# A fused two-layer decoder trunk: small loads wait for the input stream, filler matmuls follow the first real ones, token combinations go behind the first weights

## The chip, the cores and the metric

The kernel runs on one core of a Trainium2 chip. Its engines are TensorE (PE in the tables: matrix products), VectorE (DVE), ScalarE (ACT), GpSimd (POOL) and SyncE (SP, which here only issues transfers). Sixteen DMA engines move data between memory (HBM) and the on-chip buffers. The metric is the device time of one execution in microseconds (us), as the median of several runs; lower is better.

## What is computed

The reference is a trunk of two layers over 512 tokens with 1024 features, in float32. Each layer adds three parts to x; a last normalisation follows.

```python
D_MODEL = 1024; SEQ = 512; D_FF = 2816
# even layer: x += 0.5*SwiGLU(rms(x)); x += Wout[A(.) || B(.)](rms(x)); x += 0.5*SwiGLU(rms(x))
#    A = dilated sliding-window attention, B = sparse attention over indexed keys
# odd layer:  x += 0.5*SwiGLU(rms(x)); x += Wout C(rms(x)); x += 0.5*SwiGLU(rms(x))
#    C = sliding-window (128) grouped-query attention with sinks
# final RMSNorm; one relative-position bias table is added to the logits of A, B and C
```

SwiGLU(h) is (silu(h w1) * (h w3)) w2, with 2816 hidden features. So the trunk is four feed-forwards, two attentions between them and a normalisation.

## The kernel before

All of x stays on chip, as eight chunks of 128 features by 512 tokens (`self.x`). A float32 operand is split into a high and a low part (the high one is a cast by ScalarE, L336, the low one a subtraction by VectorE, L315), and a product is three matmuls: L366 to L368 in the plain form, L581 to L583 in the form with seven products.

**A feed-forward** (`ffn`) takes the 22 blocks of 128 hidden features in parts of 8, 8 and 6 (`PARTS`). The first four blocks (`PLAIN`) of the first part are computed by `gate` with plain matmuls: for each block a bank of results for w1 and one for w3, eight chunks of x by three matmuls, 24 in a bank. So there are eight plain banks. They work on x before its normalisation factor is known; `rms` finds that factor meanwhile (`newton` is its chain of small steps on VectorE), and each bank is multiplied by it afterwards (L450, L452, product L453). The other blocks come in pairs through `gates`, which forms two-by-two blocks of tokens and weights and saves one product in eight. It needs combinations of the normalised tokens (`normed`: L471 normalises a chunk, L493 adds or subtracts halves of chunks on VectorE or GpSimd, and each result is split) and of the weights (`sevens`: L533 adds halves, again on either engine). L594 copies the results out on ScalarE and L597 adds on VectorE. At the end of a part w2 is multiplied on.

**The attentions** read bias rows from a table in memory. `tables` makes it in the first feed-forward: GpSimd's queue loads its inputs, stores the rows (`rv`), and copies them shifted to `tab0` and `tab1` (the issues `tab<-rv`). A head's rows are then loaded by `toeplitz` (L661) into a buffer of kind `toep`, on SP's queue.

**The order** is a list that `Plan.emit` writes. Each operation has a due value v, the costs that the plan holds for it, and the engines that may run it; the plan repeatedly takes the engine that can start earliest and, on it, the ready operation with the least v. `CAPACITY`, `LIMIT` and `RESERVE` bound how many buffers of a kind are held. What this list fixes is the order on each engine; on the chip each engine runs its own list in order and waits by semaphores. So a transfer that can't be issued holds up all those behind it on SP's queue. `setup` issues the eight chunks of x and the first constants (ident, the identity matrix; cqg and gcol, scale vectors), and begins with a warm-up block: `WARM` = 12 matmuls on a buffer of zeros (L1045).

Of the kernel before, what the change touches and what calls it, by code (L numbers as in the profile page):

```python
# [36 lines left out]
LIMIT = {'mm': 4, 'sc': 2, 'sci': 4, 'pt': 2, 'ptv': 1, 'o': 6, 'tmp': 6, 'relu': 2, 'score': 3, 'qx': 6, 'toep': 5, 'prob': 6, 'turn': 3, 'sq': 2, 'q': 4, 'k': 4, 'vf': 3, 'of': 4, 'gt': 16, 'wraw': 6, 'cq2': 2, 'xn': 10, 'sa': 2, 'sb': 2, 'sk': 2}  # L37
RESERVE = {'q': 8, 'vf': 4, 'whl': 3, 'wraw': 5}


# [75 lines left out]
class Plan:  # L116
# [55 lines left out]
    def emit(self, make):  # L172
# [11 lines left out]
        free = {t: [0.0] * n for t, n in CAPACITY.items()}  # L184
        held, turn = {}, {}

        def offer(o):
# [4 lines left out]
        def slot_time(o):  # L192
            t, need = 0.0, {}
            for b in o.alloc:
                if held.get(b.kind, 0) + need.get(b.kind, 0) >= LIMIT.get(b.kind, 1 << 30):
                    return None
                if b.rank != turn.get(b.kind, 0) + need.get(b.kind, 0):
                    return None
                need[b.kind] = need.get(b.kind, 0) + 1
                n = need[b.tag, 0] = need.get((b.tag, 0), 0) + 1  # L200
                f = free[b.tag]
                if len(f) < n + RESERVE.get(b.kind, 0):
                    return None
                t = max(t, f[n - 1])
            return t
# [5 lines left out]
        while count < total:  # L211
# [30 lines left out]
            for b in o.alloc:  # L242
# [5 lines left out]
                b.t = make(b)  # L248
            fn()
            now[e] = st + ns  # L250
            o.fin, o.eng, o.done = st + ns + o.lat, e, True
# [16 lines left out]
class Trunk:  # L268
# [87 lines left out]
    def matmuls(self, ps, hl, rhs, m=128, c0=0, step=None):  # L356

        nc = self.nc
        n = len(rhs)
        for i, (xh, xl) in enumerate(rhs):  # L360
            c = c0 + i * (step or m)

            def f(i=i, c=c, xh=xh, xl=xl):
                o = ps.t[:m]
                wh, wl = hl.at(0, slice(c, c + m)), hl.at(1, slice(c, c + m))
                nc.tensor.matmul(o, wl, xh.t, start=i == 0, stop=False)  # L366
                nc.tensor.matmul(o, wh, xl.t, start=False, stop=False)  # L367
                nc.tensor.matmul(o, wh, xh.t, start=False, stop=i == n - 1)  # L368
            self.pe(3 * pe_ns(S), f, self.parts(hl, i, n) + [xh, xl], [ps])

    def hi(self, out, src, rows=slice(None), key=None, sb=True, n=S):
# [44 lines left out]
    def rms(self, n):  # L416
# [11 lines left out]
        def f3():  # L428
            for tb in range(4):
                nc.tensor.transpose(p2.t[:, tb * 128:(tb + 1) * 128], y.t[:, tb:tb + 1].to_broadcast([128, 128]),  # L430
                                    self.ident)
        self.pe(1000, f1, [acc, "ident"], [p1], v0)
        self.dve(2300, lambda: list(self.newton(p1.t[:, :4], y.t, n)), [p1], [y], v0)
        self.pe(450, f3, [y], [p2], v0)
        self.act(act_ns(S, False), lambda: nc.scalar.copy(r.t, p2.t), [p2], [r], v0)
# [22 lines left out]
    def normed(self, R, ncol):  # L458
# [29 lines left out]
        def comb(o, i, a, j, b, k, add=False):  # L488
# [6 lines left out]
            self.p.op([("dve", vec_ns(256), f(nc.vector)), ("pool", 750.0, f(nc.gpsimd))], keys, [(o, i)], v)  # L495
        top, low, ts = [], [], []
        for k in range(4):
# [4 lines left out]
        for k in range(4):  # L502
            low.append(norm(k + 4))
            both(["b21", "b22"], slot(), low[k], slice(0, 512), slice(0, 512), (), [low[k]])
        for k in range(4):
            a, x0, x1 = self.s2("xn"), top[k], low[k]
            ts.append(a)
            comb(a, 0, x0, 0, x0, 1)
# [338 lines left out]
    def hybrid(self, nxt):  # L847
# [13 lines left out]
        for m in range(2):  # L861
# [4 lines left out]
            self.act(act_ns(S, True, 1), lambda f=f, ch=ch, g=g: nc.scalar.activation(  # L866
                ch.t, f.t, AF.Copy, scale=g), [f, "g"], [ch])
            self.dve(dve_ns(S), lambda f=f, ch=ch, cl=cl, g=g: nc.vector.scalar_tensor_tensor(
# [160 lines left out]
    def setup(self):  # L1029
# [13 lines left out]
        ps = self.bank("ptv")  # L1043
        for _ in range(WARM):
            self.pe(427, lambda: nc.tensor.matmul(ps.t, idle[:, :128], idle, start=True, stop=True), ["idle"], [ps], v)  # L1045
        self.act(1500, lambda: nc.scalar.activation(idle2, idle[:, :1], AF.Square), ["idle"], ["idle2"], v)
        self.dma(lambda: nc.scalar.dma_start(self.gcol, t["gcol"]), (), ["g0"], 28672, v, "act")
        self.dma(lambda: nc.scalar.dma_start(self.cqg, t["cqg"]), ["g0"], ["g"], 1024, v, "act")
        self.dma(lambda: nc.scalar.dma_start(self.ident, t["ident"]), (), ["ident0"], 65536, v, "act")
        self.dve(50, lambda: nc.vector.memset(self.ones, 1.0), ["ident0"], ["ident"], v)  # L1050
        self.x = [self.s2("x") for _ in range(KD)]
        for k, x in enumerate(self.x):
            self.dma(lambda k=k, x=x: nc.sync.dma_start(x.t, t["x"][k]), (), [x], 262144, START_X[k])

    def tables(self):
# [6 lines left out]
        v = LATE  # L1062
        self.dma(lambda: pool.dma_start(self.tri, t["tri"]), (), ["tri"], 65536, v, "pool")
        self.act(250, lambda: nc.scalar.copy(self.identb, self.ident), ["ident"], ["identb"], v)
        self.dma(lambda: pool.dma_start(self.sinkp, bass.AP(
            tensor=t["sinks"].tensor, offset=t["sinks"].offset, ap=[[0, 128], [1, 16]])), (), ["sink0"], 8192, v, "pool")
        self.dve(80, lambda: nc.vector.tensor_scalar(self.sinkn, self.sinkp, -1.0, 0.0, op0=OP.mult, op1=OP.add),
                 ["sink0"], ["sink"], v)
        self.dma(lambda: pool.dma_start(tab.t, t["table"]), (), [tab], 2048, v, "pool")
        for c0, (a, n) in enumerate(((0, 512), (512, TOEP - 512))):  # L1070
            self.dma(lambda c0=c0, a=a, n=n: pool.dma_start(hot[c0].t[:, :n], t["onehot"][:, a:a + n]), (), [hot[c0]],
                     65536, v, "pool")
# [3 lines left out]
            for i in range(2):  # L1076
                ad, rs = add[2 * c0 + i], res[2 * c0 + i]
                self.dma(lambda i=i, a=a, n=n, ad=ad: pool.dma_start(ad.t[:, :n], t["addc"][:, i, a:a + n]), (), [ad],
                         32768, v, "pool")
# [69 lines left out]
    def norm_half(self, part, acc, sq):  # L1149
# [7 lines left out]
        def f1():  # L1157
            for i in range(2):
                tb = slice((2 * part + i) * 128, (2 * part + i) * 128 + 128)
                nc.tensor.matmul(p1.t[:, i:i + 1], acc.t[:, tb], self.ones, start=True, stop=False)  # L1160
                nc.tensor.matmul(p1.t[:, i:i + 1], sq.t[:, tb], self.ones, start=False, stop=True)
        self.pe(700, f1, [acc, (sq, part), "ident"], [p1], v0)
        steps = []
# [76 lines left out]
LATE = 20000.0  # L1240
WARM = 12
START_X = (-20000.0, -16900.0, -11000.0, -10900.0, -9000.0, -8900.0, -6000.0, -5900.0)

# [78 lines left out]
```

## Time and profile before

| | us |
|---|---|
| median of 3 runs | 1855.19 (1854.97 to 1855.77) |
| the profiled execution | 1856.36 |
| its span in the trace | 1854.6 |

The profiled execution is 1.76 us longer than its span, and 1.17 us above the median. Times in the trace count from the start of the span. The granted clock is given as a share: 1.00 is 2.4 GHz for TensorE and 0.50 is 1.2 GHz. A row of a timeline gives the start, the duration, engine, source line and operation, and in brackets the idle time before it with what ended it. In the trace's names `d` is a buffer of 128 x 1024, `s` one of 128 x 512, `ps` a bank of results.

### The profile page before, as it was taken

How to read it: one execution, taken by the hardware profiler on the slowest of the kernel's cores; microseconds unless marked ns; L12 is line 12 of the kernel's file. 1: busy time of each engine (PE TensorE's matmuls, PEld its weight loads, DVE VectorE, ACT ScalarE, POOL GpSimd, SP SyncE). 2: the span in 40 equal slices, each digit the busy share in tenths (PEclk: the TensorE clock that was granted, in tenths of full speed). 3: DMA queues.
4: the chain of work that ended last, by engine and by line, in shares of the span. 5: the costliest groups of instructions: out<-in, count | busy, mean ns of one | idle time of the engine just before them, and what ended most of it. 6: DMA issues, size and time to landing. Idle time of an engine off the chain costs nothing.

```text
span 1854.6 us, 28373 instructions
## 1 busy us (share of the span) xinstructions
PE 1811.5 (98%) x11174; PEld 1619.7 (87%) x11178; DVE 1398.2 (75%) x2222; ACT 936.2 (50%) x1558; POOL 245.1 (13%) x240
## 2 busy tenths in 40 slices
PE   8899999989999999999999999999999999999997
PEld 6789989867877789899998989989888889899896
DVE  7965866759998898487588965857789898567483
ACT  6443533636757746254264543525569655345153
POOL 1500001024622120010001000001023120010010
PEclk9899999999999999999999999999999999999999
DMA  6463233432222323234334223323412223243131
GB/s 210 121 207 101 84 101 106 126 103 77 87 59 78 93 71 121 62 108 132 91 103 125 69 91 103 125 70 103 137 60 69 86 80 95 78 124 126 60 112 46
DMA packets 65431, 185.45 MB, mean 100 GB/s; under 512 B 11985, under 2 KB 14769, under 8 KB 65297
## 3 DMA queue, kind: packets, MB, share of 16 engines
q1 hardware_dynamic: 58176, 176.88, 30.9%
q0 software_dynamic: 6688, 6.66, 1.3%
q8 instruction: 87, 1.43, 0.3%
q14 instruction: 48, 0.39, 0.1%
q10 hardware_dynamic: 432, 0.10, 0.0%
HBM read 179.81 MB, written 8.47 MB: 102 GB/s over the span
## 4 chain that ended last, share of the span: by engine, by line
PE 81%; DVE 12%; issue 2%; ACT 2%; DMA 2%; POOL 1%; SPq 1%; DVEq 0%; POOLq 0%; ACTq 0%
PE ps L581 12%; PE ps L582 12%; PE ps L583 12%; PE ps L366 11%; PE ps L367 11%; PE ps L368 11%; DVE d L315 3%; DVE s L315 2%; PE ps L837 1%; DMA d<-in_w 1%; PE ps L839 1%; PE ps L838 1%; PE ps L797 1%; DVE s L755 1%; DVE s L471 1%
## 5 line engine op out<-in xcount | busy, mean ns | idle before, releaser
L336 ACT CAST d<-d 128x1024 fp32r<-128x1024 f32 (+4 forms) x492 | 448.6, 927 | 405.0 <-DMA d<-in_w 223.3
L315 DVE TENSOR_TENSOR d<-d,d 128x1024 fp32r<-128x1024 f32 (+3 forms) x475 | 507.1, 1084 | 176.1 <-ACT d L336 155.0
L581 PE MATMUL ps<-s,d 128*128 128x256 f32 x2016 | 572.2, 284 | 10.9 <-DVE d L315 7.9
L582 PE MATMUL ps<-s,d 128*128 128x256 f32 x2016 | 571.5, 283 | 0.0
L583 PE MATMUL ps<-s,d 128*128 128x256 f32 x2016 | 571.4, 283 | 0.0
L366 PE MATMUL ps<-s,d 128*128 128x512 f32 x1188 | 471.8, 397 | 3.6 <-DVE d L315 3.6
L367 PE MATMUL ps<-s,d 128*128 128x512 f32 x1188 | 465.1, 392 | 0.2
L368 PE MATMUL ps<-s,d 128*128 128x512 f32 x1188 | 464.7, 391 | 0.0
L581 PEld LDWEIGHTS ps<-s,d 128*128 128x128 f32 x2016 | 388.0, 192 | 12.5 <-DVE d L315 8.2
L582 PEld LDWEIGHTS ps<-s,d 128*128 128x128 f32 x2016 | 388.0, 192 | 0.5
L583 PEld LDWEIGHTS ps<-s,d 128*128 128x128 f32 x2016 | 387.9, 192 | 0.0
L366 PEld LDWEIGHTS ps<-s,d 128*128 128x128 f32 x1188 | 224.4, 189 | 47.9 <-DVE d L315 3.8
L368 PEld LDWEIGHTS ps<-s,d 128*128 128x128 f32 x1188 | 224.0, 189 | 47.8
L367 PEld LDWEIGHTS ps<-s,d 128*128 128x128 f32 x1188 | 224.5, 189 | 42.9 <-DVE s L315 0.5
L594 ACT COPY d<-ps 128x512 f32<-128x512 f32 x144 | 84.4, 586 | 217.6 <-PE ps L583 217.5
L653 DVE SCALAR_TENSOR_TENSOR s<-ps,s 128x512 f32<-128x512 f32 x88 | 60.7, 690 | 137.0 <-PE ps L368 136.8
L315 DVE TENSOR_TENSOR s<-s,s 128x512 fp32r<-128x512 f32 (+2 forms) x188 | 148.7, 803 | 7.3 <-ACT s L372 2.1
L533 POOL TENSOR_TENSOR d<-d 128x512 f32<-128x512 f32 x18 | 23.6, 1313 | 937.1 <-DVE d L533 807.1
L597 DVE TENSOR_TENSOR d<-ps,d 128x512 f32<-128x512 f32 x108 | 73.5, 686 | 32.7 <-PE ps L583 32.1
L533 DVE TENSOR_TENSOR d<-d,d 128x512 f32<-128x512 f32 x133 | 87.5, 686 | 1.7
L533 DVE TENSOR_TENSOR d<-d 128x512 f32<-128x512 f32 x126 | 85.6, 695 | 2.2
L764 ACT ACTIVATE s<-s,stat 128x256 f32<-128x256 f32 (+3 forms) x128 | 65.9, 516 | 24.6 <-DVE stat L755 23.9
(147 smaller groups left out, 1872.0 us busy)
## 6 DMA issues: line engine op xcount, KB each, us to landing
d<-in_w SPq DMA_DIRECT2D x234, 512.0 KB, 3.7
d<-in_w SPq DMA_DIRECT2D x32, 384.0 KB, 3.2
d<-in_hyb_in SPq DMA_DIRECT2D x22, 512.0 KB, 3.9
d<-in_swa_in SPq DMA_DIRECT2D x10, 512.0 KB, 3.6
tab<-rv POOLq DMA_DIRECT2D x4, 1024.0 KB, 16.7
s<-tab SPq DMA_DIRECT2D x16, 256.0 KB, 4.0
d<-in_hyb_out SPq DMA_DIRECT2D x16, 256.0 KB, 2.9
d<-in_swa_out SPq DMA_DIRECT2D x16, 256.0 KB, 2.7
```

The lines of the kernel that those rows point to most:

```text
L315: return lambda: eng.tensor_sub(out(), a(), b().bitcast(F32))
L336: alts = [("act", ns[0](n), lambda: nc.scalar.copy(hl.at(0, o), raw.t[:, c]))]
L366: nc.tensor.matmul(o, wl, xh.t, start=i == 0, stop=False)
L367: nc.tensor.matmul(o, wh, xl.t, start=False, stop=False)
L368: nc.tensor.matmul(o, wh, xh.t, start=False, stop=i == n - 1)
L533: return lambda: eng.tensor_add(o.t[:, oc], a.t[:, ac], o.t[:, oc])
L581: nc.tensor.matmul(o, wl, xh, start=start and m == 0 and k == 0, stop=False, skip_group_check=True)
L582: nc.tensor.matmul(o, wh, xl, start=False, stop=False, skip_group_check=True)
L583: nc.tensor.matmul(o, wh, xh, start=False, stop=k == 3, skip_group_check=True)
L594: self.act(sca_ns(S) - 40, lambda: nc.scalar.copy(view(q, c), bank(ps)), [ps], [(q, key)])
L597: self.dve(vec_ns(S), lambda: nc.vector.tensor_add(view(q, c), bank(ps), view(q, c)), [ps, (q, key)], [(q, key)])
L764: nc.scalar.activation(x, x, AF.Exp, bias=st.t[:, qb:qb + 1], scale=-1.0, accum_out=st.t[:, 4 + qb:5 + qb])
```

## The change

There are five edits. A `toep` buffer is handed out only if its load is due at most 30 us (30000 in the plan's units) after the latest matmul that was put on the list (`AHEAD`, `front`). Six more matmuls on zeros (`FILL`) follow the first three real ones, in the bank of the warm-up block. The token combinations in `normed` get a due value 22 us later, in all four feed-forwards. The loads of ident and cqg move from ScalarE's queue to GpSimd's, and with those of tri, sinks, table, onehot and addc wait until the sixth chunk of x has landed. The memset of the ones no longer waits for ident.

```diff
+AHEAD = {'toep': 30000.0}
...
+                if b.kind in AHEAD and o.v > front + AHEAD[b.kind]:
+                    return None
...
             fn()
+            if e == "pe":
+                front = max(front, o.v)
...
             self.pe(3 * pe_ns(S), f, self.parts(hl, i, n) + [xh, xl], [ps])
+            if self.warm and i == 0:
+
+                self.warm(FILL, self.parts(hl, i, n) + [xh, xl], self.vt)
+                self.warm = None
...
+
+        v += 22000.0
         for k in range(4):
             a, x0, x1 = self.s2("xn"), top[k], low[k]
-            ts.append(a)
             comb(a, 0, x0, 0, x0, 1)
...
-        self.dma(lambda: nc.scalar.dma_start(self.cqg, t["cqg"]), ["g0"], ["g"], 1024, v, "act")
-        self.dma(lambda: nc.scalar.dma_start(self.ident, t["ident"]), (), ["ident0"], 65536, v, "act")
-        self.dve(50, lambda: nc.vector.memset(self.ones, 1.0), ["ident0"], ["ident"], v)
+        self.dve(50, lambda: nc.vector.memset(self.ones, 1.0), (), ["ones"], v)
...
-            self.dma(lambda k=k, x=x: nc.sync.dma_start(x.t, t["x"][k]), (), [x], 262144, START_X[k])
+            self.dma(lambda k=k, x=x: nc.sync.dma_start(x.t, t["x"][k]), (), [x, ("landed", k)], 262144, START_X[k])
+
+        self.dma(lambda: nc.gpsimd.dma_start(self.ident, t["ident"]), [("landed", 5)], ["ident"], 65536, 0.0, "pool")
...
-        self.dma(lambda: pool.dma_start(self.tri, t["tri"]), (), ["tri"], 65536, v, "pool")
+        after = [("landed", 5)]
+        self.dma(lambda: pool.dma_start(self.cqg, t["cqg"]), after, ["cqg"], 1024, v, "pool")
+        self.dma(lambda: pool.dma_start(self.tri, t["tri"]), after, ["tri"], 65536, v, "pool")
...
+FILL = 6
```

The plan decides the rest, so the order on the engines is shown at three places. Numbers in the names tell buffers apart and differ between the two kernels; line numbers of the changed kernel are higher by 7 to 17.

On TensorE, at the end of the warm-up block, three real matmuls followed one another before, on one bank:

```order
L1045 MATMUL ps<-idle 128x512
L366 MATMUL ps<-s_125,d_122 128x512
L367 MATMUL ps<-s_131,d_114 128x512
L368 MATMUL ps<-s_125,d_114 128x512
L366 MATMUL ps<-s_125,d_137 128x512
L367 MATMUL ps<-s_131,d_129 128x512
L368 MATMUL ps<-s_125,d_129 128x512
```

Now the first three (L373 to L375) are followed by six on zeros (two are shown, each with its weight load):

```order
L1058 MATMUL ps<-idle 128x512
L373 MATMUL ps<-s_102,d_117 128x512
L374 MATMUL ps<-s_110,d_107 128x512
L375 MATMUL ps<-s_102,d_107 128x512
L1058 LDWEIGHTS idle
L1058 MATMUL ps<-idle 128x512
L1058 LDWEIGHTS idle
L1058 MATMUL ps<-idle 128x512
```

The fills stand between the first chunk of x and the next matmul; before, that next matmul worked on the w3 weight with the same chunk.

On VectorE, ahead of the first products of `gates`, the split of the second weight (w3, a row of L315 with 128x1024) stood at place 77, after token combinations (L493) and their splits:

```order
L493 TENSOR_TENSOR s_535<-s_501,s_460 128x256
L315 TENSOR_TENSOR s_538<-s_486,s_519 128x512
L315 TENSOR_TENSOR s_543<-s_489,s_540 128x512
L493 TENSOR_TENSOR s_535<-s_535,s_460 128x256
L315 TENSOR_TENSOR s_563<-s_491,s_558 128x512
L315 TENSOR_TENSOR s_568<-s_499,s_565 128x512
L315 TENSOR_TENSOR s_574<-s_501,s_570 128x512
L1080 TENSOR_TENSOR s_579<-s_510,ps 16x512
L315 TENSOR_TENSOR d_583<-d_297,d_398 128x1024
```

Now it stands at place 70, after the rescaling of one more plain bank pair (L461 to L464, before L450 to L453):

```order
L482 SCALAR_TENSOR_TENSOR s_484<-s_160,gcol,s_376 128x512
L1097 TENSOR_TENSOR s_499<-s_255,ps 16x512
L461 TENSOR_TENSOR s_508<-ps,s_376 128x512
L463 TENSOR_TENSOR s_514<-ps,s_376 128x512
L322 TENSOR_TENSOR s_520<-s_484,s_506 128x512
L464 TENSOR_TENSOR s_514<-s_508,s_514 128x512
L322 TENSOR_TENSOR d_537<-d_295,d_413 128x1024
L322 TENSOR_TENSOR s_547<-s_514,s_539 128x512
```

On TensorE all eight plain banks now stand ahead of the first product (L593); before, 48 products stood between the sixth and the seventh. The w1 split of the second group of `gates` is VectorE's 93rd row before and its 99th now.

On SP's queue, in the first feed-forward, loads of bias rows (L661) stood between the weights (L328):

```order
L328 DMA d_692<-in_w 128x1024
L661 DMA s_858<-tab_69 128x512
L328 DMA d_875<-in_w 128x1024
L661 DMA s_893<-tab_69 128x512
L661 DMA s_908<-tab_69 128x512
L661 DMA s_911<-tab_69 128x512
L328 DMA d_927<-in_w 128x1024
```

Now only weights (L335) stand there:

```order
L335 DMA d_755<-in_w 128x1024
L335 DMA d_764<-in_w 128x1024
L335 DMA d_895<-in_w 128x1024
L335 DMA d_961<-in_w 128x1024
L335 DMA d_981<-in_w 128x1024
```

The first loads of bias rows moved to just before the first attention uses them, and those of the other table to the second attention's input projections.

## Rows read from the trace of the kernel before

**Rows 1.** The page: TensorE's busy time, its share of the span, instructions.

```profile
PE 1811.5 (98%) x11174; PEld 1619.7 (87%) x11178; DVE 1398.2 (75%) x2222; ACT 936.2 (50%) x1558; POOL 245.1 (13%) x240
```

**Rows 2.** TensorE's waits over the span: total us, times, longest.

```profile
PE ps L581 <- DVE d L315: 7.9, 1, 7.9
```

**Rows 3.** Timeline of TensorE, 0 to 17 us: start, duration.

```profile
1.20 5.07 PE L1045 MATMUL ps<-idle 128*128 128x512 bf16 x12 [1.20 <-DVE ones L1050]
...
7.43 0.39 PE L368 MATMUL ps<-s,d 128*128 128x512 f32 x1
11.15 0.80 PE L366 MATMUL ps<-s,d 128*128 128x512 f32 x1 [3.32 <-DVE d L315]
...
16.30 0.40 PE L366 MATMUL ps<-s,d 128*128 128x512 f32 x1
16.54 0.39 PE L367 MATMUL ps<-s,d 128*128 128x512 f32 x1
```

**Rows 4.** Timeline of ScalarE, 0 to 16 us.

```profile
9.75 0.62 ACT L336 CAST d<-d 128x512 fp32r<-128x512 f32 x1 [3.50 <-DMA d<-in_w]
```

**Rows 5.** DMA, 0 to 16 us: GB/s by 0.4 us; an issue, us to landing.

```profile
GB/s 0 0 0 0 41 134 364 362 300 379 254 217 141 89 105 85 171 264 222 247 247 323 391 410 394 307 302 384 353 405 410 394 405 384 384 384 389 379 384 364
...
tri<-in_tri POOLq DMA_DIRECT2D x1, 64.0 KB, 5.2
```

**Rows 6.** Windows: length; busy us of PE, PEld, DVE, ACT, POOL; clock; DMA share; GB/s.

```profile
4.00:7.20 3.20, 2.85 (x8) 0.90 (x7) 1.38 (x2) 1.44 (x3) 0.11 (x1) 1.00 0.92 166
...
10.00:16.00 6.00, 4.85 (x11) 3.81 (x12) 5.04 (x9) 5.31 (x10) 0.00 (x0) 0.50 1.05 375
...
31.80:72.85 41.05, 33.17 (x158) 27.47 (x157) 39.15 (x53) 20.00 (x33) 26.43 (x23) 0.88 0.10 30
...
450.00:550.00 100.00, 96.66 (x488) 79.77 (x488) 99.12 (x254) 58.68 (x130) 52.13 (x47) 1.00 0.25 76
```

**Rows 7.** Timeline of TensorE, 59 to 76 us.

```profile
59.13 0.58 PE L581 MATMUL ps<-s,d 128*128 128x256 f32 x1 [7.88 <-DVE d L315]
59.51 0.41 PE L582 MATMUL ps<-s,d 128*128 128x256 f32 x1
...
63.77 0.35 PE L581 MATMUL ps<-s,d 128*128 128x256 f32 x1
...
75.63 0.28 PE L581 MATMUL ps<-s,d 128*128 128x256 f32 x1
75.74 0.28 PE L582 MATMUL ps<-s,d 128*128 128x256 f32 x1
```

**Rows 8.** Timeline of VectorE, 28 to 78 us.

```profile
31.80 2.36 DVE L315 TENSOR_TENSOR d<-d,d 128x1024 fp32r<-128x1024 f32 x2
...
34.78 0.68 DVE L452 TENSOR_TENSOR s<-ps,s 128x512 f32<-128x512 f32 x1
35.38 0.74 DVE L471 SCALAR_TENSOR_TENSOR s<-s,gcol,s 128x512 f32<-128x512 f32 x1
...
42.48 1.22 DVE L471 SCALAR_TENSOR_TENSOR s<-s,gcol,s 128x512 f32<-128x512 f32 x1
...
70.58 2.34 DVE L315 TENSOR_TENSOR d<-d,d 128x1024 fp32r<-128x1024 f32 x2
```

**Rows 9.** Timeline of SP's queue, 0 to 100 us.

```profile
11.68 52.84 SPq L328 DMA_DIRECT2D d<-in_w  x17
88.70 0.33 SPq L661 DMA_DIRECT2D s<-tab  x1
```

**Rows 10.** Timeline of ScalarE, 95 to 104 us.

```profile
101.77 1.05 ACT L336 CAST d<-d 128x1024 fp32r<-128x1024 f32 x1 [1.57 <-DMA d<-in_w]
```

**Rows 11.** TensorE's waits, 0 to 110 us: total, times, longest.

```profile
PE ps L581 <- ACT d L594: 1.7, 2, 1.0
```

**Rows 12.** Timeline of TensorE at 1543 us.

```profile
1543.39 0.39 PE L581 MATMUL ps<-s,d 128*128 128x256 f32 x1 [1.30 <-ACT d L594]
```

**Rows 13.** Waits of SP's queue over the span: total, times, longest.

```profile
SPq L328 <- DVE d L315: 541.7, 99, 18.3
```

More of the change, by code (lines that the diff above doesn't have):

```diff
@@ L185, in emit @@
         held, turn = {}, {}
+        front = -1.0e9
         def offer(o):
@@ L431, in f3 @@
                                     self.ident)
-        self.pe(1000, f1, [acc, "ident"], [p1], v0)
+        self.pe(1000, f1, [acc, "ones"], [p1], v0)
         self.dve(2300, lambda: list(self.newton(p1.t[:, :4], y.t, n)), [p1], [y], v0)
-        self.pe(450, f3, [y], [p2], v0)
+        self.pe(450, f3, [y, "ident"], [p2], v0)
         self.act(act_ns(S, False), lambda: nc.scalar.copy(r.t, p2.t), [p2], [r], v0)
@@ L495, in comb @@
             self.p.op([("dve", vec_ns(256), f(nc.vector)), ("pool", 750.0, f(nc.gpsimd))], keys, [(o, i)], v)
-        top, low, ts = [], [], []
+        top, low = [], []
         for k in range(4):
@@ L866, in hybrid @@
             self.act(act_ns(S, True, 1), lambda f=f, ch=ch, g=g: nc.scalar.activation(
-                ch.t, f.t, AF.Copy, scale=g), [f, "g"], [ch])
+                ch.t, f.t, AF.Copy, scale=g), [f, "cqg"], [ch])
             self.dve(dve_ns(S), lambda f=f, ch=ch, cl=cl, g=g: nc.vector.scalar_tensor_tensor(
@@ L1043, in setup, with warm @@
         ps = self.bank("ptv")
-        for _ in range(WARM):
-            self.pe(427, lambda: nc.tensor.matmul(ps.t, idle[:, :128], idle, start=True, stop=True), ["idle"], [ps], v)
+        def warm(n, r, v):
+            for _ in range(n):
+                self.pe(427, lambda: nc.tensor.matmul(ps.t, idle[:, :128], idle, start=True, stop=True), ["idle", *r], [ps], v)
+        self.warm = warm
+        warm(WARM, (), v)
         self.act(1500, lambda: nc.scalar.activation(idle2, idle[:, :1], AF.Square), ["idle"], ["idle2"], v)
-        self.dma(lambda: nc.scalar.dma_start(self.gcol, t["gcol"]), (), ["g0"], 28672, v, "act")
-        self.dma(lambda: nc.scalar.dma_start(self.cqg, t["cqg"]), ["g0"], ["g"], 1024, v, "act")
-        self.dma(lambda: nc.scalar.dma_start(self.ident, t["ident"]), (), ["ident0"], 65536, v, "act")
-        self.dve(50, lambda: nc.vector.memset(self.ones, 1.0), ["ident0"], ["ident"], v)
+        self.dma(lambda: nc.scalar.dma_start(self.gcol, t["gcol"]), (), ["g"], 28672, v, "act")
+        self.dve(50, lambda: nc.vector.memset(self.ones, 1.0), (), ["ones"], v)
         self.x = [self.s2("x") for _ in range(KD)]
         for k, x in enumerate(self.x):
-            self.dma(lambda k=k, x=x: nc.sync.dma_start(x.t, t["x"][k]), (), [x], 262144, START_X[k])
+            self.dma(lambda k=k, x=x: nc.sync.dma_start(x.t, t["x"][k]), (), [x, ("landed", k)], 262144, START_X[k])
+        self.dma(lambda: nc.gpsimd.dma_start(self.ident, t["ident"]), [("landed", 5)], ["ident"], 65536, 0.0, "pool")
     def tables(self):
@@ L1062, in tables @@
         v = LATE
-        self.dma(lambda: pool.dma_start(self.tri, t["tri"]), (), ["tri"], 65536, v, "pool")
+        after = [("landed", 5)]
+        self.dma(lambda: pool.dma_start(self.cqg, t["cqg"]), after, ["cqg"], 1024, v, "pool")
+        self.dma(lambda: pool.dma_start(self.tri, t["tri"]), after, ["tri"], 65536, v, "pool")
         self.act(250, lambda: nc.scalar.copy(self.identb, self.ident), ["ident"], ["identb"], v)
         self.dma(lambda: pool.dma_start(self.sinkp, bass.AP(
-            tensor=t["sinks"].tensor, offset=t["sinks"].offset, ap=[[0, 128], [1, 16]])), (), ["sink0"], 8192, v, "pool")
+            tensor=t["sinks"].tensor, offset=t["sinks"].offset, ap=[[0, 128], [1, 16]])), after, ["sink0"], 8192, v, "pool")
         self.dve(80, lambda: nc.vector.tensor_scalar(self.sinkn, self.sinkp, -1.0, 0.0, op0=OP.mult, op1=OP.add),
                  ["sink0"], ["sink"], v)
-        self.dma(lambda: pool.dma_start(tab.t, t["table"]), (), [tab], 2048, v, "pool")
+        self.dma(lambda: pool.dma_start(tab.t, t["table"]), after, [tab], 2048, v, "pool")
         for c0, (a, n) in enumerate(((0, 512), (512, TOEP - 512))):
-            self.dma(lambda c0=c0, a=a, n=n: pool.dma_start(hot[c0].t[:, :n], t["onehot"][:, a:a + n]), (), [hot[c0]],
+            self.dma(lambda c0=c0, a=a, n=n: pool.dma_start(hot[c0].t[:, :n], t["onehot"][:, a:a + n]), after, [hot[c0]],
                      65536, v, "pool")
@@ L1077, in tables @@
                 ad, rs = add[2 * c0 + i], res[2 * c0 + i]
-                self.dma(lambda i=i, a=a, n=n, ad=ad: pool.dma_start(ad.t[:, :n], t["addc"][:, i, a:a + n]), (), [ad],
+                self.dma(lambda i=i, a=a, n=n, ad=ad: pool.dma_start(ad.t[:, :n], t["addc"][:, i, a:a + n]), after, [ad],
                          32768, v, "pool")
@@ L1161, in f1 @@
                 nc.tensor.matmul(p1.t[:, i:i + 1], sq.t[:, tb], self.ones, start=False, stop=True)
-        self.pe(700, f1, [acc, (sq, part), "ident"], [p1], v0)
+        self.pe(700, f1, [acc, (sq, part), "ones"], [p1], v0)
         steps = []
```

## The prediction

> **What bounds the kernel now.** I read the page first: TensorE (PE) is busy for 98% of the span [rows 1]. So a change can win only where PE waits or runs at the lower of its two clocks, and I went to PE's waits next: the list by line, for the span, comes to some 30 us, and one wait makes 7.9 of them [rows 2]. Then I followed each wait that the edits touch back to what is late. The reader is to see three places.
>
> The start: PE's first three real matmuls end at 7.83, and the next starts at 11.15 [rows 3]. ScalarE sat 3.50 us waiting for a weight, till 9.75 [rows 4]. The DMA engines were busy all that time, but the rate sank to 85 to 141 GB/s in four slices of 0.4 us, where it is near 390 later [rows 5]. The small loads are in flight there: 64 KB of tri took 5.2 us. From 10 to 16 us the granted clock is 0.50 [rows 6], that is 1.2 GHz, after the 3.32 us gap; the twelve matmuls from 11.15 to 16.30 stand 0.43 apart, then 0.23 [rows 3].
>
> The first feed-forward: PE stops at 51.25 for 7.88 us and comes back at half clock, 0.213 us a product for 21 products, against 0.12 later [rows 7]. What it waited for is the w3 split that VectorE (DVE) did just ahead of 59.13; the order shows it behind token combinations.
>
> The second half of that stage: SP issues nothing from 64.5 to 88.70, where a toep load waits for its table [rows 9]; three w2 weights are issued behind it. ScalarE then waits for w2, once 1.57 us [rows 10]; a copy (L594) stands behind those casts, and two waits of PE on that copy make 1.7 us of the first 110 [rows 11].
>
> **The change part by part.** *Start.* The small loads leave the first 5 us; they start when the sixth chunk of x is there. With no slump a 256 KB piece should land every 0.65 us (390 GB/s [rows 5]), so the weight needed at 9.73 comes near 5.5. PE's first real matmul hangs on the warm-up block, which ends at 6.27 [rows 3], and hardly moves. Six fills follow: at 0.213 (half of the 0.42 that the twelve at 1.2 GHz took, 5.07/12 [rows 3]) 1.3 us, at 0.42 2.5 us. The matmul that began at 16.30 is the 16th; 7.83 + 1.3 + 12 x 0.23 = 11.9. So the start gains 4.4, and with the first matmul 0.2 earlier 4.6. Bounds: 1.0, if the fills don't hold the clock (twelve matmuls at 0.43 and fills at 0.42 give back 3.6), and 5.0.
>
> *Token combinations behind the first weights.* In the new order the w3 split stands at DVE's 70th place and not at its 77th, so the 7.88 us wait goes. But all eight plain banks (192 matmuls) now stand ahead of the first product, before it were six, and DVE evacuates two more banks early. What is late next is the second weight group: its w1 split was DVE's 93rd row and is its 99th. Before, from the end of the newton steps at 31.80 to the end of that split at 71.72, which is the first of the two from 70.58 [rows 8], DVE took 39.9 us; in this stretch it was nearly always busy (39.15 of 41.05 us [rows 6]). The new list has four more rescalings of a bank (L450, L452) and one more multiplication (L453), two more splits of 512, one more small subtraction, one weight sum of two halves more and two in-place ones less, no L597: at 0.6 from start to start [rows 8] that is 4 x 0.6 + 0.6 + 2 x 0.6 + 0.2 - 0.6 - 0.6 = 3.2. So the split ends 43.1 us after newton, which ends at 31.80 - 4.6 = 27.2: 70.3. PE could be there at 75.63 - 4.6 - 7.9 - 2.0 = 61.1 (2.0: the 21 slow products at 0.093 more each). So there is a new wait, of some 9 us, in place of the old one, and the clock falls again. The products of the second group start at 70.3 and not at 75.63 [rows 7], 5.3 earlier; the half-clock stretch, which was over by 75.63, is now still to come: less 2.0, a gain of **3.3**.
>
> The unknown in this is how much GpSimd (POOL) slows DVE. With POOL idle an L471 took 0.74 us, with POOL at its combinations 1.22 [rows 8], and POOL was busy 26.43 of the 41.05 us [rows 6]. Instruction by instruction, against those of the same kind with POOL idle, I count some 7.7 us of such excess in the old stretch. Its combinations are the same twelve, so I leave it as it is. Bounds: an excess of 2 us gives 5.7 more, one of 13 takes 5.3 off. The Trainium skill's page "SBUF — State Buffer", section "SBUF: two separate sides", states that a DVE instruction with two SBUF inputs and a GpSimd one share a port pair that one holds for its whole instruction while the other is blocked. By that rule moving the combinations can't remove the excess, only put it elsewhere; the rows agree as far as they go, and a sum by the rule, with each of twelve combinations holding DVE for its own 1.2 us, would put the split at about 77, no gain.
>
> The other three feed-forwards get the same offset. In the one at 1500 a copy stands behind two casts and PE waits 1.30 [rows 12]; the copy moves ahead of them: **1.3**, bounds 0 and 1.3.
>
> *Toep buffers near the front.* SP's block of 24 us goes, since no toep load is left in the first feed-forward; what hid behind it, the w2 weights, come early, and the two waits on the copy go [rows 11]: **1.7**, bounds 0 and 1.7. The loads go to 360 to 380 us and, for the other table, to the second attention. There SP's queue is in order, and a weight ahead of a toep load waits for its buffer, up to 18.3 us [rows 13]. I cost it at nothing: what covers it is the 30 us by which they are let in ahead of PE. Small swaps in the first attention (450 to 550, DVE busy 99.12 of 100 us [rows 6]) have no cover there: between -3 and +3, taken at 0.
>
> Sum: 3.3 + 1.3 + 1.7 = 6.3 us. The profiled execution took 1856.36 with a span of 1854.6; that is 1.17 above the median of the runs, so I take the sum off the median: 1855.19 - 6.3 = **1848.9**.
>
> **Rivals.**
> (1) *The start gains and DVE eats it.* The second group's split comes at 73.6 or later (73.6 + 2.0 = 75.63): the excess would have to be 11 us. For it: POOL has an add more in this stage, and DVE rows 82 to 99, about 10 us, wait for banks of the last plain part. Against it: POOL's combinations are as many as before. Then only 1.3 + 1.7 remain: 1852.2, and with one of these missing no difference.
> (2) *The slump moves and does not go.* The Trainium skill's page "DMA: Bandwidth & Descriptors", section "Issuing engines are not separate DMA queues", states that transfers of all engines run on the same 16 DMA engines and interleave, so that a queue change alone frees nothing. As a mechanism of this kernel: the slump cost (375 - 166) GB/s x 3.2 us [rows 6], 0.67 MB or 1.8 us of stream, and after the sixth chunk it falls on the weights of the second plain bank, needed at 18 to 24 us. Against it: SP fetches those weights well ahead of need once nothing holds it. If so, the start gains 2.8, the sum is 4.5, the time 1850.7.
> (3) *Slower: one toep load is stuck.* In the second attention a toep load issued behind a weight that waits for its buffer comes too late. SP's longest such wait is 18.3 us [rows 13]; if PE meets all of it: 18.3 - 6.3 = 12.0, 1867. It decides from 10 us of lateness on. For it: before, those loads were done hundreds of us ahead. Against it: 30 us ahead of PE is more than 18.3, and PE has other work there.
> (4) *Better.* The excess on DVE is small since its w3 split and evacuations run while POOL still waits: split at 64 to 66, the wait at the second group 3 to 5 us, the clock mostly kept: 5 more, 1844.
>
> **How the numbers follow.** A difference under 0.2%, 3.7 us, is about what a measurement of this kernel can't tell from none: the edges are 1851.5 and 1858.9. Chances: my forecast 0.42 and (2) 0.11, nearly all of it faster; (4) 0.14, faster; (1) 0.18, nearly all within 0.2%; (3), with all other ways of losing (the swaps at 450 to 550), 0.15, slower. Faster 0.66, same 0.18, slower 0.16. The range must reach over (4) and its bound (-5.7 on DVE) below, and over (1) above up to the bound of 13 us of excess with the swaps at +3: 1855.19 - 6.3 + 5.3 + 3 = 1857. So 1842 to 1857; the forecast's own, 1845 to 1851.5.
>
> **What would show it.** Right: the second real piece starts within 2 us of the first and the granted clock is 1.00 from 10 to 16; PE's wait before the first product is under 2 us and a wait of 6 to 11 us stands before the second group, on a DVE split, with half clock behind it; no SP block until 88; no PE wait at 99 and 103, nor in the feed-forward at 1500. Wrong: half clock at 10 to 16; a wait of over 13 us before the second group; any PE wait over 2 us in the attentions on a toep load.

## Result and the profile after

The changed kernel takes 1872.68 us (median of 4 runs, 1871.31 to 1873.73), the kernel before 1855.08 in the same job: a ratio of 1.0094 [1.0077, 1.0112], 17.6 us **slower**, where 6.3 us faster was forecast. The span of the profiled execution went from 1854.6 to 1871.1, by 16.5.

I looked for the place first. The table has the starts of TensorE's pieces in the two timelines: the first product of a feed-forward, and the next plain matmul (there w2 begins). Between them stand the product pairs of the first part.

| | before | after | shift there |
|---|---|---|---|
| first feed-forward, second group of products | 75.63 | 72.25 | -3.4 |
| first feed-forward, products of the second part | 156.72 | 159.29 | +2.6 |
| second, first product / w2 | 693.93 / 734.26 | 696.38 / 740.96 | +2.5 / +6.7 |
| third, first product / w2 | 1040.25 / 1080.58 | 1046.77 / 1094.47 | +6.5 / +13.9 |
| fourth, first product / w2 | 1536.18 / 1578.05 | 1550.01 / 1594.51 | +13.8 / +16.5 |

The attentions between them shift nothing. All is lost in four stretches of some 40 us, in each just after the products begin: 6.0 us in the first feed-forward, after a gain of 3.4, and 4.2, 7.4 and 2.6 in the others.

**The start.** The rows that answer to [rows 6], then GpSimd's timeline from 0 to 6 us:

```profile
4.00:7.20 3.20, 3.00 (x11) 1.20 (x10) 1.35 (x2) 1.10 (x2) 1.17 (x3) 1.00 0.92 242
10.00:16.00 6.00, 5.22 (x14) 3.34 (x14) 5.29 (x9) 5.22 (x9) 0.00 (x0) 0.72 1.05 360
```

```profile
1.29 0.77 POOL L1068 DMA_DIRECT2D ident<-in_ident  x1 [0.84 <-POOLq L1329]
...
4.68 0.49 POOL L1095 DMA_DIRECT2D s<-in_addc  x1
```

Ident is issued at 1.29 us and the last of these seven loads at 4.68, while the sixth chunk of x is not even asked for (SP issues the fifth and the sixth from 4.75 on). **No load waits.** What the title and the section on the change say of a wait for the sixth chunk holds for the plan's list, not for the chip. The rate between 4 and 7.2 us is 242 GB/s (166 before, 375 in the steady stretch), and the clock still falls for part of the stretch from 10 to 16.

**The product blocks.** TensorE's waits over the span (the two longest groups), which answer to [rows 2], and its timeline at the ends of three of them, which answer to [rows 7]:

```profile
PE ps L593 <- ACT d L606: 14.4, 4, 4.6
PE ps L593 <- DVE d L322: 8.0, 1, 8.0
```

```profile
14.77 0.62 PE L373 MATMUL ps<-s,d 128*128 128x512 f32 x1
...
72.25 0.55 PE L593 MATMUL ps<-s,d 128*128 128x256 f32 x1 [8.05 <-DVE d L322]
...
99.11 0.58 PE L593 MATMUL ps<-s,d 128*128 128x256 f32 x1 [4.53 <-ACT d L606]
...
1057.24 0.58 PE L593 MATMUL ps<-s,d 128*128 128x256 f32 x1 [4.56 <-ACT d L606]
```

The wait on a split ahead of the second group is the one that was forecast. The four on a copy (L606, L594 before) were not. To see why the copy is late I followed it back. First feed-forward, GpSimd, VectorE and ScalarE in turn:

```profile
71.31 7.55 POOL L1105 DMA_DIRECT2D tab<-rv  x7
89.03 1.09 POOL L1105 DMA_DIRECT2D tab<-rv  x1 [10.16 <-issue]
90.13 1.30 POOL L545 TENSOR_TENSOR d<-d 128x512 f32<-128x512 f32 x1
```

```profile
91.47 2.50 DVE L545 TENSOR_TENSOR d<-d,d 128x512 f32<-128x512 f32 x4 [6.24 <-POOL d L545]
```

```profile
94.60 1.99 ACT L343 CAST d<-d 128x1024 fp32r<-128x1024 f32 x2 [5.15 <-DVE d L545]
...
98.49 0.56 ACT L606 COPY d<-ps 128x512 f32<-128x512 f32 x1
```

GpSimd issues seven of the eight table copies, stands 10.16 us before the eighth, and only then adds one pair of weight halves (L545). VectorE's next sums wait for that add, ScalarE's casts for the sums, and the copy that would free TensorE's bank stands behind the casts. Behind that wait TensorE's products stand 0.21 us apart until 103.5, at half clock, and 0.12 later. In the kernel before, GpSimd's last sum of the first part ran at 67.68 us, ahead of its first copy at 72.83.

In the third feed-forward GpSimd has other work in front. Its timeline, and VectorE's:

```profile
1036.50 1.22 POOL L504 TENSOR_TENSOR s<-s,s 128x256 f32<-128x256 f32 x1 [0.53 <-ACT s L525]
1037.69 1.73 POOL L545 TENSOR_TENSOR d<-d 128x512 f32<-128x512 f32 x1
1040.10 1.62 POOL L545 TENSOR_TENSOR d<-d 128x512 f32<-128x512 f32 x1 [0.69 <-issue]
1041.80 3.31 POOL L545 TENSOR_TENSOR d<-d,d 128x512 f32<-128x512 f32 x2
```

```profile
1038.20 1.77 DVE L322 TENSOR_TENSOR d<-d,d 128x512 fp32r<-128x512 f32 x1
...
1042.20 1.77 DVE L545 TENSOR_TENSOR d<-d,d 128x512 f32<-128x512 f32 x1
...
1045.59 0.68 DVE L545 TENSOR_TENSOR d<-d,d 128x512 f32<-128x512 f32 x1
```

Four sums of weights follow the token combinations on GpSimd; before, it had no work there from 1030 to 1060 us. Beside these sums an operation of 128x512 on VectorE takes 1.77 us (the split at 1038.20, the add at 1042.20); alone, 0.68. This holds throughout this trace: of the 514 two-operand operations of 128x512 on VectorE that touch no bank of results and have no such operation of GpSimd beside them, none takes over 0.92 us; of the 95 with one, half take 1.22 or more. GpSimd was given 29 sums in all before and 45 after, and 14 of the 16 new ones are in the last three feed-forwards.

### The profile page after: what moved, and what is told of

The parts are those of the page before. It is cut to its first block, busy times and chain, and to the rows that moved or that the text cites. A ratio compares the mean times of both kernels' runs of the same rounds, so it can differ in the third digit from the quotient of the medians.

```text
span 1871.1 us, 28424 instructions
## 1 busy us (share of the span) xinstructions
PE 1819.2 (97%) x11184; PEld 1626.7 (87%) x11184; DVE 1402.4 (75%) x2194; ACT 937.2 (50%) x1556; POOL 289.0 (15%) x272
## 4 chain that ended last, share of the span: by engine, by line
PE 74%; DVE 14%; issue 4%; ACT 3%; DMA 3%; POOL 2%; SPq 0%; DVEq 0%; POOLq 0%; ACTq 0%
PE ps L593 12%; PE ps L594 12%; PE ps L595 12%; PE ps L373 9%; PE ps L375 9%; PE ps L374 9%; DVE d L322 3%; DVE s L322 3%; PE ps L849 1%; PE ps L851 1%; PE ps L850 1%; DVE s L482 1%; DMA tab<-rv 1%; DVE s L767 1%; PE ps L809 1%
## 5 line engine op out<-in xcount | busy, mean ns | idle before, releaser
L593 PE MATMUL ps<-s,d 128*128 128x256 f32 x2016 | 576.1, 286 | 22.4 <-ACT d L606 14.4
L594 PE MATMUL ps<-s,d 128*128 128x256 f32 x2016 | 575.1, 285 | 0.0
L373 PE MATMUL ps<-s,d 128*128 128x512 f32 x1188 | 472.0, 397 | 0.8 <-ACT s L394 0.6
L375 PE MATMUL ps<-s,d 128*128 128x512 f32 x1188 | 464.6, 391 | 0.0
L593 PEld LDWEIGHTS ps<-s,d 128*128 128x128 f32 x2016 | 391.6, 194 | 23.9 <-ACT d L606 15.2
L594 PEld LDWEIGHTS ps<-s,d 128*128 128x128 f32 x2016 | 391.6, 194 | 0.5
L375 PEld LDWEIGHTS ps<-s,d 128*128 128x128 f32 x1188 | 223.8, 188 | 47.8
L373 PEld LDWEIGHTS ps<-s,d 128*128 128x128 f32 x1188 | 224.3, 189 | 45.4 <-ACT s L394 1.7
L606 ACT COPY d<-ps 128x512 f32<-128x512 f32 x144 | 84.4, 586 | 239.7 <-PE ps L595 235.7
L545 POOL TENSOR_TENSOR d<-d 128x512 f32<-128x512 f32 x27 | 38.6, 1431 | 918.5 <-DVE d L545 633.6
L322 DVE TENSOR_TENSOR s<-s,s 128x512 fp32r<-128x512 f32 (+2 forms) x189 | 159.9, 857 | 7.8 <-ACT s L383 5.0
L545 DVE TENSOR_TENSOR d<-d,d 128x512 f32<-128x512 f32 x126 | 84.8, 699 | 7.7 <-POOL d L545 6.2
L545 DVE TENSOR_TENSOR d<-d 128x512 f32<-128x512 f32 x117 | 79.0, 687 | 2.2
```

The source lines that it names most:

```text
L322: return lambda: eng.tensor_sub(out(), a(), b().bitcast(F32))
L545: return lambda: eng.tensor_add(o.t[:, oc], a.t[:, ac], o.t[:, oc])
L593: nc.tensor.matmul(o, wl, xh, start=start and m == 0 and k == 0, stop=False, skip_group_check=True)
L594: nc.tensor.matmul(o, wh, xl, start=False, stop=False, skip_group_check=True)
L606: self.act(sca_ns(S) - 40, lambda: nc.scalar.copy(view(q, c), bank(ps)), [ps], [(q, key)])
```

## Experiments

The kernel before was timed along with each job: 1856.1, 1856.0, 1855.6 and 1855.5 us. Profiles of one kernel differ by a few us from execution to execution, so I compare ratios for the whole and the lengths of the product blocks for a place. The last three columns are the lengths in us from the first product to w2, in the second, third and fourth feed-forward; the sums are counted on GpSimd's list.

| kernel | ratio to before | median | sums on GpSimd | 2nd | 3rd | 4th |
|---|---|---|---|---|---|---|
| before | 1 | | 29 | 40.33 | 40.33 | 41.87 |
| the change | 1.0094 [1.0077, 1.0112] | 1872.68 | 45 | 44.58 | 47.70 | 44.50 |
| e1_no_offset | 1.0011 [1.0002, 1.0021] | 1859.07 | 35 | 41.75 | 44.53 | 41.86 |
| e2_offset_first | 1.0031 [1.0019, 1.0043] | 1862.12 | 37 | 41.74 | 43.04 | 41.88 |
| e3_offset_alone | 1.0043 [1.0028, 1.0058] | 1863.98 | 42 | 42.16 | 42.14 | 43.28 |
| e4_ahead_alone | 1.0027 [1.0017, 1.0036] | 1861.34 | 35 | 41.75 | 43.04 | 41.87 |
| e5_start_alone | 0.9983 [0.9974, 0.9993] | 1852.62 | 29 | 40.31 | 40.31 | 41.89 |
| e6_start_no_fill | 0.9997 [0.9988, 1.0006] | 1854.97 | 29 | 40.32 | 40.31 | 42.10 |
| e7_copies_later | 1.0067 [1.0050, 1.0084] | 1867.98 | 45 | 44.66 | 46.62 | 43.26 |
| e9_sums_on_dve | 1.0029 [1.0018, 1.0040] | 1862.35 | 11 | 41.05 | 42.14 | 41.03 |
| e10_sums_no_offset | 1.0036 [1.0023, 1.0048] | 1862.98 | 9 | 42.49 | 42.82 | 42.65 |
| e11_real_wait | 0.9979 [0.9970, 0.9988] | 1851.63 | 29 | 40.33 | 40.32 | 41.86 |
| e12_ahead_first | 0.9995 [0.9986, 1.0004] | 1855.23 | 29 | 40.33 | 40.32 | 41.88 |
| e13_wait_copies | 0.9970 [0.9959, 0.9982] | 1849.52 | 27 | 40.33 | 40.32 | 41.88 |
| e14_copy_dve | 1.0098 [1.0082, 1.0113] | 1872.67 | 22 | 42.41 | 42.37 | 42.55 |
| e15_offset_held | 1.0032 [1.0020, 1.0043] | 1861.41 | 44 | 42.15 | 42.15 | 44.78 |

**Which edit costs.** e1 takes the offset out of the changed kernel, e2 leaves it in the first feed-forward alone, e3 adds it alone to the kernel before, e4 adds the rule for toep buffers alone, e5 is the start alone (e3 to e5 consist of lines of the change).

```diff
-        v += 22000.0                         # e1
+        if self.vt < 30000:                  # e2
+            v += 22000.0
```

> The changed kernel without the 22 us offset of the token combinations; start, fills and the rule for toep buffers stay. Theory A (the offset puts the combinations of a feed-forward into the time of the weight sums, which then wait on POOL's list behind them; all of the loss is there): the four product blocks are as before, the 7.88 us wait ahead of the first w3 split is back, the start gains 4.5 and the w2 waits 1.7: about 1849, bounds 1847 to 1852. Theory B (the rule for toep buffers frees buffers, the plan then fetches and sums weights earlier and overloads POOL): the waits at 702, 1053 and 1556 stay, 1865 or more.

> The changed kernel with the offset in the first feed-forward alone. A: the product blocks of the other three feed-forwards, which lost 4.25, 7.37 and 2.63 us, are as before: 1872.7 - 14.3 = 1858.4, bounds 1856 to 1860; the waits at 64 and 95 us stay. B: the later waits stay, 1868 or more.

> The kernel before with the offset as its only change. A: 14 us lost in the last three feed-forwards, and in the first a sum of weights behind the table copies on POOL, some 5 to 8 us, less what the earlier w3 split gives: 1869 to 1877. B: within 3 us of the kernel before.

> The kernel before with the rule for toep buffers as its only change. POOL's list then has 35 sums of weights and not 29, the same as in the run without the offset. C (each edit that lets the plan put more sums on POOL costs in the product blocks behind them): the second and third feed-forward lose 1.4 and 4.2 us as in that run, the first gains some 2: 1857 to 1860. A (only the offset costs): 1853.

> The small loads behind the sixth chunk and the six fills alone, neither the offset nor the rule for toep buffers. POOL's list of sums is that of the kernel before (29). C: the product blocks of the last three feed-forwards are as before and the start's 4.5 us come through to the end: 1851.5 on this day's scale (1856 before), bounds 1850 to 1853.5. If an earlier start is lost again at the w3 split in the first feed-forward, whose time VectorE sets: 1855.

Theory A, that the offset does it all, fell with e1: without the offset 15 us of the loss go, but the kernel stays 2 us above before, not 6 below, and waits in the second and third feed-forward remain. e2 was 4 us above its 1858.4 for the same reason, e3 with 8 us lost 5 less than A's least. Theory B, that the rule for toep buffers does it all, fell too: e3 has no rule and loses. Theory C, that each edit that gives GpSimd more sums costs in the blocks behind them, had at most 1860 for e4, which came 1.3 us above: the rule alone costs 5 us, 4.1 of them in the same two blocks. In e5 the last three blocks have the old length and the kernel is 3.4 us faster, 1 us less than C had it. Not all of that can be put down to the start. Its profile is 1.4 us ahead of the kernel before at 155.37 us (products of the second part) and gains 1.8 more in the first attention, a stretch whose length differs by up to 2.5 us between the profiles here (from the first feed-forward's last w2 to the second one's first product, 350.0 to 352.6 us).

**Offset and rule together.** e12 has the rule in the first feed-forward alone, so that later toep loads are taken early and their buffers stay held; e15 is the changed kernel with the same limit.

```diff
-                if b.kind in AHEAD and o.v > front + AHEAD[b.kind]:
+                if b.kind in AHEAD and front < 400000 and o.v > front + AHEAD[b.kind]:
```

> The kernel before with the rule for toep buffers in the first feed-forward alone; later loads are taken early as before, so their buffers are held through the second and third feed-forward. POOL's list of sums is then that of the kernel before. E (it is the freed buffers that change the later order): the second and third feed-forward are as before, 40.3 us each for the four product pairs, no wait at 697 and 1047, 4 to 6 us less than the rule alone (1861.3): 1856. If the rule acts through the first feed-forward: 1860 or more.

> The changed kernel with the rule for toep buffers in the first feed-forward alone. If the two costs only add: 1872.7 less the 1.4 and 2.7 us by which the rule alone lengthens the second and third block: 1868, with the blocks at 43.2 and 45. If they work on each other (the offset's run alone had 42.16 and 42.14, both together 44.58 and 47.70): blocks near 42.2, some 8 us less, 1864.

The blocks came as expected; e15's total was 2.6 us below its 1864. In e12 the lists of TensorE, VectorE, ScalarE and GpSimd and the blocks of the second and third feed-forward are those of before. What differs there is how long five toep buffers are held. Before, and in e12, the second attention's first five loads of bias rows are issued at 568 to 603 us and their buffers stay held through both feed-forwards. In the changed kernel and in e4 these loads come from 1320 us on, and no kernel issues such a load in between. So it is the freed buffers that change the plan there, as theory E has it. In e4 the second feed-forward then gets the longer block that the fourth had all along (41.75 and 41.87, with a wait of 1.2 or 1.3 us on a copy some 7 us behind the first product), the third one longer still. In e15 the two blocks take 42.15 each, 8.0 us less than in the changed kernel (44.58 + 47.70). The rule alone adds 4.1 to them (e4), the offset alone 3.6 (e3), the two together 11.6: they strengthen each other.

**Are the sums on GpSimd the cause?** e9 keeps the sums of the last three feed-forwards on VectorE in the changed kernel, e10 in e1.

```diff
-            self.p.op([("dve", vec_ns(512), f(nc.vector)), ("pool", 1300.0, f(nc.gpsimd))],
-                      [(o, i), (a, j)], [(o, i)], v + 1000)
+            alts = [("dve", vec_ns(512), f(nc.vector)), ("pool", 1300.0, f(nc.gpsimd))]
+            self.p.op(alts[:1] if self.vt > 400000 else alts, [(o, i), (a, j)], [(o, i)], v + 1000)
```

> The changed kernel with the sums of weights of the last three feed-forwards on VectorE alone; all else stays, the offset too. C: the waits at 702, 1053 and 1556 go and with them 12 to 14 us: 1858 to 1860 (1872 before this edit). If VectorE itself is the limit there, it gets longer by the sums that POOL did (33 at 0.6 us, part of it hidden): 1868 or more.

> The run without the offset, with the sums of weights of the last three feed-forwards on VectorE alone. C: its waits at 697, 1045 and 1545 (1.2, 2.5 and 1.3, and 1.7 of half clock) go: 1859 - 6.5 = 1852.5. If VectorE is the limit: 1858 or more.

With the offset, in the main yes. TensorE's waits in e9 from 640 to 1100 us:

```profile
PE ps L593 <- DVE d L322: 1.9, 4, 0.5
PE ps L593 <- ACT d L606: 0.8, 1, 0.8
```

Of 7.1 us of waiting on the copy 0.8 are left, and the three blocks are 12.6 us shorter, of the 14.2 by which they had grown; later parts, where VectorE now does all the sums, lose 0.7 us each. The total was 2 to 4 us above what I expected. So the sums on GpSimd are what costs. How long TensorE waits goes not with their number in the whole list, which is 44 in e15, but with how many stand in the 13 us ahead of a block's first product: none in the three blocks of e9 (waits on the copy of 0 to 0.8 us), three in e3 and e15 and in two blocks of the changed kernel (1.6 to 2.7), four in its third feed-forward (4.6). That they cost by slowing VectorE beside them, and not only by coming late themselves, is read from the rows above and no run separates the two. Without the offset, no: e10 missed, its waits on the copy stay (1.2, 1.5, 1.3; in e1 1.2, 2.5, 1.3), and it is slower than e1. So most of the rule's cost has another cause. In e1 the copy stands behind two casts of the next weights; TensorE's wait, then ScalarE:

```profile
1047.49 0.38 PE L592 MATMUL ps<-s,d 128*128 128x256 f32 x1 [2.47 <-ACT d L605]
```

```profile
1044.98 1.98 ACT L343 CAST d<-d 128x1024 fp32r<-128x1024 f32 x2
1046.86 0.57 ACT L605 COPY d<-ps 128x512 f32<-128x512 f32 x1
```

e14 was to test that: the rule alone (e4), with the copies on VectorE.

```diff
-            self.act(sca_ns(S) - 40, lambda: nc.scalar.copy(view(q, c), bank(ps)), [ps], [(q, key)])
+            self.p.op([("dve", vec_ns(S), lambda: nc.vector.tensor_copy(view(q, c), bank(ps)))], [ps], [(q, key)], self.vt)
```

> The rule for toep buffers alone, with the copies of the product banks on VectorE and not on ScalarE. With the rule alone TensorE waits 1.2 and 2.5 us in the second and third feed-forward for such a copy, which stands behind casts of weights on ScalarE. F (the place behind the casts is the cause): no wait on a copy there that is over 0.6 us, 40.3 to 41 us for each of the two blocks in place of 41.75 and 43.04. If the weights themselves are late (VectorE has 144 copies more): the waits stay as waits on a split, 42 us or more.

It settles nothing: the copies then stand behind VectorE's splits, TensorE waits 1.6 for them, and 144 copies cost VectorE time everywhere. That the place behind the casts is the rule's cost is argued from the trace, not shown.

**The queue behind the table copies.** e7 is the changed kernel with the copies planned behind the first part.

```diff
+                x.t, ps.t, 0.5, x.t, op0=OP.mult, op1=OP.add), [ps, x], [x] + [("part", f0)] * (dm == KD - 1))
...
+                    [("rv", i, 0), ("rv", i, 1), ("part", 0)], [("tab", n, h // 4)], 4 * 128 * n * 4, v, "pool")
```

> The changed kernel with the copies of the shifted table held back until the first part of the first feed-forward is done, so that the one weight sum stands ahead of them on POOL's list. If that queue is the cause of the wait at 94.6: 4.5 us of wait and 3.4 us from the half clock behind it go, 1872.7 - 7.9 = 1864.8. If VectorE is late there anyway (it had 6.2 us of waiting only because it had nothing else): under 3 us, 1870 or more.

The wait that ended at 99.11 is gone, and the products end at 107.98 and not at 115.74: 7.8 us, as expected. But the next products of the first feed-forward start at 157.52 (159.29 in the changed kernel), so 6 of them are given back: the copies now run from 84 us on, when w2 is loaded. The total was 3 us above the 1864.8. DMA issues from 80 to 125 us in e7:

```profile
d<-in_w SPq DMA_DIRECT2D x10, 512.0 KB, 8.0
tab<-rv POOLq DMA_DIRECT2D x4, 1024.0 KB, 18.9
```

**The start.** e6 is e5 without the fills. In e11 GpSimd first copies one column of the sixth chunk; that copy can't start before the chunk has landed. e13 is e11 with the table copies behind the second part, as in e7 with ("part", 8).

```diff
+        mark, x5 = c.tile([128, 1], F32, name="mark"), self.x[5]
+        self.p.op([("pool", 100.0, lambda: nc.gpsimd.tensor_copy(mark, x5.t[:, :1]))], [x5], ["mark"], -1000.0)
-        self.dma(lambda: nc.gpsimd.dma_start(self.ident, t["ident"]), [("landed", 5)], ["ident"], 65536, 0.0, "pool")
+        self.dma(lambda: nc.gpsimd.dma_start(self.ident, t["ident"]), ["mark"], ["ident"], 65536, 0.0, "pool")
```

> The moved small loads alone, without the six fills. In the run with both, the second real piece began at 7.92, the fills ended just before, and the granted clock still fell to 0.50 for 3.4 us at 11.9. If the fills do nothing: as that run (1852.6, before 1856.0). If they keep the clock up for a while: the clock falls earlier and for 6.8 us, some 1.5 us more: 1854.

> Moved small loads and fills, with a wait that the chip sees: GpSimd copies one column of the sixth chunk before it issues ident, cqg, tri and the rest. In the changed kernel ident was issued at 1.29 us and no load waited. D (the slump comes from these loads): the fourth matmul starts by 8 and the 16th by 12.5, the clock holds, 2 to 3 us better than the run without the real wait: 1850. If the stream is slow for another reason (few pieces in flight at first): the weight for w3 still lands after 8, no change, 1852.6.

> The run with the real wait, and the copies of the shifted table planned behind the second part of the first feed-forward, so that they run on POOL after 180 us and not from 70 on, when w2 is loaded. The w2 weights land in 4 us, no wait at 101 us and no half clock behind it, 2 to 3.5 us less than the run with the real wait alone: 1847. If the copies disturb the weights of the second part as much: no gain.

GpSimd's timeline of e11, its windows (as [rows 6]), and TensorE's 16th real matmul:

```profile
11.33 0.18 POOL L1068 COPY mark<-s 128x1 f32<-128x1 f32 x1 [10.88 <-DMA s<-in_x]
11.46 0.78 POOL L1069 DMA_DIRECT2D ident<-in_ident  x1
```

```profile
4.00:7.20 3.20, 2.86 (x12) 1.17 (x11) 1.41 (x2) 1.63 (x3) 0.00 (x0) 1.00 0.96 343
10.00:16.00 6.00, 5.71 (x24) 4.35 (x24) 5.99 (x10) 5.83 (x10) 4.04 (x8) 1.00 1.04 383
```

```profile
12.10 0.39 PE L373 MATMUL ps<-s,d 128*128 128x512 f32 x1
```

Now the slump is gone (343 GB/s, 294 in e13) and the 16th matmul starts at 12.10 (11.91 in e13); the prediction had 11.9. In the eight runs with the change's start and no real wait it starts at 13.71 to 14.99, and the rate from 4 to 7.2 us is 208 to 265 GB/s. So the slump comes from the small loads, as theory D has it. The clock holds at 1.00 from 10 to 16 us in both runs with the wait, but that it does so by the wait is not shown: of the eight without it, whose lists begin alike, it fell in four (the changed kernel, e1, e2, e5) and held in four (e7, e9, e10, e15). The same window in e15:

```profile
10.00:16.00 6.00, 5.01 (x20) 3.43 (x20) 5.52 (x9) 5.73 (x10) 0.00 (x0) 1.00 1.05 401
```

The total of e11 is 1 us better than e5's and not 2 to 3, less than these intervals tell apart.

What the fills are worth stays open. By the ratios e6, without them, is some 2.5 us slower than e5 (1.5 expected), but the two intervals overlap, and the trace doesn't put the loss where the fills are: in e6 23 matmuls ran from 10 to 16 us at a granted 0.80, in e5 12 at 0.72, and the 16th real matmul starts at 13.37, in e5 at 14.99. What is later in e6 is VectorE's first split behind the newton steps, at 30.22 and not at 29.31.

e13 is faster than both kernels, 6 us under before; its interval and e11's overlap. DMA issues from 80 to 125 us in e11, then in e13, and the copies on GpSimd in e13:

```profile
d<-in_w SPq DMA_DIRECT2D x11, 512.0 KB, 6.5
```

```profile
d<-in_w SPq DMA_DIRECT2D x12, 512.0 KB, 3.6
```

```profile
185.64 7.59 POOL L1106 DMA_DIRECT2D tab<-rv  x7
204.68 1.09 POOL L1106 DMA_DIRECT2D tab<-rv  x1 [11.45 <-issue]
```

With the copies out of the way w2 lands in 3.6 us and not in 6.5, and TensorE has no wait from 85 to 130 us, where e11 has 2.8 us on the copy. The total was 2.5 us above its 1847. The 11.45 us stand of GpSimd is still there; its next work is a sum at 309.81 us.

## Why the prediction was wrong

- **"The small loads leave the first 5 us; they start when the sixth chunk of x is there."** This step failed first. It was read from the diff. The key ("landed", 5) is known to the plan alone; the issue carries no wait on the chip, and GpSimd's list begins with these loads. Their 16th matmul comes at 14.77, 1.5 us earlier and not 4.4. That an edit does less than it says was not among my rivals here. With a real wait (e11) the sum's term of 4.4 measured 4.2.
- **"The products of the second group start at 70.3."** They start at 72.25, the wait before them was 8.05 where I had 9, and the clock fell behind it. VectorE's first row behind the newton steps, and the split that TensorE waits for:

```profile
29.61 2.36 DVE L322 TENSOR_TENSOR d<-d,d 128x1024 fp32r<-128x1024 f32 x2
...
70.89 1.21 DVE L322 TENSOR_TENSOR d<-d,d 128x1024 fp32r<-128x1024 f32 x1
```

From 29.61 to the end of that split are 42.5 us, where the sum has 43.1. So the chain on VectorE was right, and the miss is the start's: the newton steps end 2.2 us earlier than before and not 4.6.

- **What comes next in that feed-forward** I took from the waits of before. The two waits on the copy went, as said; in their place came one of 4.53 us and a stretch at half clock, from a single sum of weights that the new order puts behind the table copies. The order had that row; I read POOL's list only up to the second group.
- **"The other three feed-forwards get the same offset ... 1.3."** Here the sign was wrong, and most of the loss is here: 14.2 us by the blocks (5.1 with the offset alone, e3; 4.1 with the rule alone, e4). The copy did not move ahead of late casts: the wait of 1.30 at 1543 became one of 2.68 at 1558.60. Moving the combinations 22 us later put them next to the sums of weights, and the plan gave GpSimd the sums, at a cost of 1.3 us each and none for VectorE's slow-down; with these sums back on VectorE (e9) 12.6 of the 14.2 go. I worked out this contention for the first feed-forward and did not ask for it in the others.
- **"I cost it at nothing"**, of the rule for toep buffers: it costs some 5 us alone. I asked what a late load costs (rival 3; no attention lost anything) and not what the freed buffers do to the plan.
- The rule of the Trainium skill's page "SBUF — State Buffer", section "SBUF: two separate sides" (of a DVE instruction with two SBUF inputs and a GpSimd one, the first to start holds a shared port pair for its whole instruction, and the other is blocked) pointed at the right place. The 1.77 us of a VectorE add beside a GpSimd add, 0.68 alone, agree with it, as a wait of about one us for the other.

## What to carry to other kernels

A list scheduler can make an edit global: moving one group of operations, or freeing buffers, can change which engine gets work hundreds of us away (here it did; the start alone, e5, changed nothing in the later blocks). Count in the order, for each stage, what each engine was given, before costing an edit at its own place. A dependence that only the planner knows is no wait on the chip: look for the wait on the instruction itself. And work given to a second engine to relieve the first isn't free when the two slow each other, nor when it stands in a queue behind transfers.

## What the runs showed that I had not expected

In the seven runs in which all eight table copies stand in a row (the changed kernel, e2, e3, e7, e9, e13, e15), GpSimd issues seven of them back to back and stands 8.5 to 11.5 us before the eighth (10.16 in the changed kernel, 11.45 in e13). In each of the seven it goes on about 0.5 us after the first of the copies has landed. In the changed kernel that copy, issued at 71.31, is also the quickest, with 17.2 us to landing, at 88.5; the eighth is issued at 89.03:

```profile
DMA to landing us min/median/max: 17.2/21.7/26.9
```

Transfers of 512 KB for w2 took 6.5 us to land beside these copies in e11 and 8.0 in e7, and 3.6 without them (e13).

The clock at the start can't be read from one profile. In the four runs in which it fell, the longest gap between two matmuls from 5.5 us to the fall was 0.30 to 0.79 us (0.40 in the changed kernel); in the four with the same list in which it held, the longest up to 18 us was 0.40 to 0.65. So the longest gap alone doesn't tell the two apart.
